# Five raw weight buffers, a first norm with channel factors as 128x8 values, and another order at the phase boundaries

## The chip, the core and the metric

The kernel runs on one core of a Trainium2 chip. The metric is the device time of one execution in microseconds (us), the median of some runs. Four compute engines matter: TensorE (PE in the profile; PEld are its weight loads), VectorE (DVE), ScalarE (ACT) and GpSimd (POOL). SyncE (SP) issues almost every DMA. Each engine works through its own instructions strictly in their order; semaphores order the engines among each other.

## The reference, cut to what matters

Everything is float32, x is 256 tokens of 1024 channels. Two layers of a first block with three branches, then two layers of a second block (a mixer and a feed-forward network):

```python
def first_block(x, mem, ...):
    for l in range(DEPTH):
        h = rms_norm(x, norm_g[l])
        q_a, k_a, v_a, q_h, f_h, i_h, q_m, z = split(h @ w_in[l])
        o_a = moba_attention(rope(norm(q_a)), rope(norm(k_a)), v_a)   # 8 heads of 64
        o_h = rms_norm(hgrn2_chunkwise(q_h, f_h, i_h, lb[l]), hgrn_o_norm[l])
        kv_m = rms_norm(mem, mem_norm_g[l]) @ w_mem_kv[l]             # mem: 256 x 1024
        k_m, v_m = split(kv_m)
        o_m = memory_attention(norm(q_m), norm(k_m), v_m)             # 4 heads of 128
        x = x + (concat([o_a, o_h, o_m]) * silu(z)) @ w_out[l]
    return x

def second_block(x, ...):
    for l in range(DEPTH):
        m = hybrid_mixer(rms_norm_2(x, mix_pre_norm[l]), ...)         # delta net, retention, pooling
        x = x + rms_norm_2(m, mix_post_norm[l])
        h = rms_norm_2(x, ffn_pre_norm[l])
        x = x + rms_norm_2((silu(h @ gate[l]) * (h @ up[l])) @ down[l], ffn_post_norm[l])
    return x
```

`rms_norm(x, g)` divides each token's row by its root mean square and multiplies by the channel gain `g`. Since `mem` is the same for both layers, the two memory norms differ only in that gain.

## The kernel before, in words

**Tiling.** x is two tiles of 128 tokens. A norm makes `xn` of a tile, TensorE transposes it against the identity (8 blocks of 128x128, written into two PSUM banks `mx`), and the result is split into a rounded part and a remainder, `aTh` and `aTl`: that is `hT`, the input of the next phase. Weights come in units of 512 KB (128x1024), 420 in all. Each unit is requested by SP into a buffer `raw`, split into `wh` (a cast on ScalarE) and `wl = raw - wh` (a subtraction on VectorE), and each product is three matmuls, high by high, low by high, high by low, summed in a PSUM bank `acc` or `mx`. The number behind `raw`, `wh`, `wl` in a name is the unit's.

**The weight stream** (class `Stream`, L228 to L327). There are RAW = 3 raw buffers and SLOTS = 6 split buffers; units marked so may take up to SPARE = 2 more from the pool `k4`. `pump` (L292) requests the next raw unit as soon as an earlier raw buffer's second split is issued (`n_dma - n_l < RAW`), and issues splits up to AHEAD = 6 units ahead while a slot is free. `take` hands a unit to the matmuls, `free` gives its slot back.

**The order** is made while the program is built, by a planner (class `Order`, L149, with `Engine`, L98). It keeps an estimate of TensorE's time and of when each tile will be ready, from costs per engine. Work that depends on other work (norms, evacuations, attention, softmaxes) is written as generators that yield what they wait for. After every three matmuls `poll` runs each generator whose tile is due within SLACK = 200 ns of TensorE's estimate, so its instructions fall in there. `join` moves the estimate forward until a named generator is done. The estimate decides only the order in each queue; the real waits are semaphores.

**Phases.** `tok` (L577) makes token-tile outputs, first tile 0 for all keys, then tile 1. `chan` does the same by channels. `out_proj` (L629) sums a product over several units into four banks, two for each tile; its last SKEW units run for tile 0 first and then for tile 1, so that tile 0's residual, norm and transposes can run under tile 1's matmuls. In layer 0 of the first block the order is i_h, f_h, q_h, q_a, k_a, v_a, km, vm, q_m, z1, z0, z2; in layer 1 km and vm come first. The memory is normed once in each layer (`mem_norm`, L811) and `mem_kv` makes its keys and values. The two HGRN chains (`hgrn`, L954; `hZ` is a decayed operand of its matmuls, made after a `TENSOR_TENSOR_SCAN`) and the four softmaxes (`softmax_pv`, L1028, two of MoBA and two of the memory) run as generators beside the projections.

**Start** (`run`, L1710). SP requests x's two tiles, the identity, the gain row `norm_g` broadcast to 128 partitions, then weight units 0, 1, 2. `norm` (L509) squares a tile (`junk`, with the sum as a side output), makes `r` (the small steps `y`), multiplies the tile by `r` and the gain (`xn`, L109 is the helper that records every planned operation), and transposes it.

The gain multiplication and the stream's pace setters in code:

```python
        for xc, gc in zip(self.halves(x), self.halves(gb)):
            xn.append(self.k2([P, 512], "xn"))
            self.dve.scalar_tensor_tensor(xn[-1], xc, r, gc, op0=ALU.mult, op1=ALU.mult)
...
        while self.n_dma < len(self.units) and self.n_dma - self.n_l < self.RAW:
            self._dma()
        if (self.n_h < min(self.n_dma, self.at + self.AHEAD) and self._can_place()
                and o.when(self.raw[self.n_h]) <= o.pe + o.SLACK):
            self._split_h()
```

## Time and profile before

| what | us |
|---|---|
| time before, median of 3 runs (1424.21 to 1426.77) | 1424.57 |
| the profiled execution, whole time | 1426.05 |
| its span in the profile | 1424.3 |
| TensorE busy (97% of the span) | 1386.4 |
| VectorE busy (71%) | 1014.8 |
| ScalarE busy (58%) | 832.2 |
| GpSimd busy (2%) | 23.7 |

The profiled execution takes 1.75 us more than its span, and 1.48 us more than the median of the runs. The profile is read from the whole to the part: the busy time of each engine, the same by stretches of the span, then in a stretch what each engine waited for. A busy time tells nothing of the clock, so the granted clock (PEclk, as a share of full speed) is read beside it.

### The profile page before, as it was taken

What the parts mean: (1) busy time and instruction counts of PE and PEld (TensorE: products, weight loads), DVE (VectorE), ACT (ScalarE), POOL (GpSimd) and SP (SyncE); (2) the same over time, 40 slices, a digit from 0 to 9 for tenths busy, and PEclk for the clock granted to TensorE, in tenths of its full rate; (3) what the DMA queues carried; (4) which work ended last, traced back from release to release, by engine and by line L of the source; (5) the groups of instructions that cost most, each with busy time, mean ns of one, the idle gap of its engine ahead of it and who ended that gap; (6) DMA issues with size and microseconds to landing.
All of it is one profiled execution on the core that took longest, in us unless ns stands there. A gap on an engine that the chain in (4) does not pass through costs nothing.

```text
span 1424.3 us, 20430 instructions
## 1 busy us (share of the span) xinstructions
PE 1386.4 (97%) x7620; PEld 1167.8 (82%) x7620; DVE 1014.8 (71%) x1693; ACT 832.2 (58%) x1415; POOL 23.7 (2%) x65
## 2 busy tenths in 40 slices
PE   7999999999999999999999999999999999999998
PEld 6778887888887898888877888779888887788886
DVE  5887778589777698657777655677958677765554
ACT  5856666576675476556656554555656556555453
POOL 6000000000000000000000000000000000000000
PEclk9999999999999999999999999999999999999999
DMA  8752555554257464235664666745543366566662
GB/s 273 163 179 60 150 191 192 178 155 142 77 155 247 127 180 136 84 104 177 186 221 141 193 190 193 222 120 150 168 126 118 91 193 220 162 191 192 181 190 89
DMA packets 139524, 231.67 MB, mean 163 GB/s; under 512 B 26272, under 2 KB 32032, under 8 KB 139424
## 3 DMA queue, kind: packets, MB, share of 16 engines
q1 hardware_dynamic: 139392, 230.36, 53.6%
q8 instruction: 60, 0.98, 0.3%
q14 instruction: 40, 0.33, 0.1%
q0 software_dynamic: 32, 0.00, 0.0%
HBM read 229.28 MB, written 1.05 MB: 162 GB/s over the span
## 4 chain that ended last, share of the span: by engine, by line
PE 74%; DVE 9%; DMA 9%; ACT 5%; issue 3%; SPq 0%; DVEq 0%; ACTq 0%
PE acc L135 52%; PE mx L135 18%; PE mx L145 4%; DVE wl L109 4%; DMA raw<-in_w_in 3%; ACT wh L109 3%; DMA raw<-in_w_out 2%; DMA raw<-in_ffn_down 1%; DMA raw<-in_ffn_up 1%; ACT sg L109 1%; DVE aTl L109 1%; ACT junk L109 0%; DMA mem<-in_mem 0%; DVE zc L109 0%; DMA x<-in_x 0%
## 5 line engine op out<-in xcount | busy, mean ns | idle before, releaser
L109 DVE TENSOR_TENSOR wl<-raw,wh 128x1024 fp32r<-128x1024 f32 x412 | 502.5, 1222 | 196.6 <-ACT wh L109 191.7
L109 ACT CAST wh<-raw 128x1024 fp32r<-128x1024 f32 x412 | 431.2, 1049 | 258.1 <-PE acc L135 80.8
L135 PE MATMUL acc<-wh,aTh 128*128 128x512 f32 x1232 | 492.5, 400 | 2.3 <-ACT aTh L109 2.3
L135 PE MATMUL acc<-wh,aTl 128*128 128x512 f32 x1232 | 485.4, 394 | 1.2 <-DVE aTl L109 1.2
L135 PE MATMUL acc<-wl,aTh 128*128 128x512 f32 x1232 | 485.8, 394 | 0.2 <-DVE wl L109 0.2
L135 PEld LDWEIGHTS acc<-wh,aTl 128*128 128x128 f32 x1232 | 231.9, 188 | 50.4 <-DVE aTl L109 2.9
L135 PEld LDWEIGHTS acc<-wh,aTh 128*128 128x128 f32 x1232 | 232.4, 189 | 47.9 <-ACT aTh L109 3.1
L135 PEld LDWEIGHTS acc<-wl,aTh 128*128 128x128 f32 x1232 | 232.4, 189 | 45.8 <-issue 1.0
L135 PE MATMUL mx<-wh,ff 128*128 128x512 f32 x352 | 112.6, 396 | 0.0
L135 PE MATMUL acc<-aTh,wh 128*128 128x256 f32 x320 | 91.1, 285 | 0.0
L135 PE MATMUL acc<-aTl,wh 128*128 128x256 f32 x320 | 90.6, 283 | 0.0
L135 PE MATMUL acc<-aTh,wl 128*128 128x256 f32 x320 | 90.5, 283 | 0.0
L135 PEld LDWEIGHTS mx<-wh,ff 128*128 128x128 f32 x352 | 66.3, 190 | 13.5
L109 ACT ACTIVATE sg<-sg 128x512 f32<-128x512 f32 (+1 forms) x120 | 73.9, 615 | 1.7
L109 ACT ACTIVATE sg<-zc 128x512 f32<-128x512 f32 (+1 forms) x60 | 36.9, 614 | 63.5 <-DVE zc L109 63.5
L135 PE MATMUL mx<-wl,ff 128*128 128x512 f32 x176 | 69.2, 393 | 0.0
L135 PEld LDWEIGHTS acc<-aTh,wh 128*128 128x128 f32 x320 | 61.3, 192 | 0.3
L135 PEld LDWEIGHTS acc<-aTh,wl 128*128 128x128 f32 x320 | 61.3, 192 | 0.2
L135 PEld LDWEIGHTS acc<-aTl,wh 128*128 128x128 f32 x320 | 61.3, 192 | 0.0
L109 DVE TENSOR_SCALAR zc<-acc 128x512 f32<-128x512 f32 (+1 forms) x48 | 31.8, 662 | 22.5 <-PE acc L135 22.5
L109 ACT CAST aTh<-mx 128x512 fp32r<-128x512 f32 x52 | 28.9, 585 | 26.2 <-PE mx L145 25.9
L135 PEld LDWEIGHTS mx<-wl,ff 128*128 128x128 f32 x176 | 33.5, 190 | 7.1
(304 smaller groups left out, 1588.5 us busy)
## 6 DMA issues: line engine op xcount, KB each, us to landing
raw<-in_w_in SPq DMA_DIRECT2D x200, 512.0 KB, 4.1
raw<-in_ffn_down SPq DMA_DIRECT2D x44, 512.0 KB, 4.7
raw<-in_w_out SPq DMA_DIRECT2D x40, 512.0 KB, 4.8
raw<-in_ffn_gate SPq DMA_DIRECT2D x40, 512.0 KB, 4.3
raw<-in_ffn_up SPq DMA_DIRECT2D x40, 512.0 KB, 3.9
raw<-in_w_mem_kv SPq DMA_DIRECT2D x16, 512.0 KB, 4.6
raw<-in_w_branch_pool SPq DMA_DIRECT2D x8, 512.0 KB, 4.5
raw<-in_w_branch_ret SPq DMA_DIRECT2D x8, 512.0 KB, 4.7
```

The lines of the kernel that those rows point to most:

```text
L109: r = f(out, *args, **kw)
L135: self._ns.matmul(out, lhsT, rhs, **kw)
L145: self._ns.transpose(out, x, ident)
```

## The change

- **Sizes.** Five raw buffers instead of three, paid for by one buffer less in the pool `k4` and two less in `k2`. SKEW is 4 instead of 3.
- **Planner.** A scan counts twice its columns, and an instruction whose bias or scale is a tile counts 70 ns more.
- **First norm of x.** It multiplies by `r` alone. Its gain comes as a 128x8 tile `gain0` (channel k*128+p at partition p, column k, fetched by GpSimd's queue), and since the transposed blocks have channels on partitions, the gain is the scale of the split: eight ScalarE copies of 128x128 for `aTh` and eight VectorE operations for `aTl` of each tile, where there were two and two.
- **Memory.** It is normed once, without a gain. The gains of both layers come as 128x8 tiles `memgain0` and `memgain1` and go into the splits of the 16 memory weight units, two halves of 512 columns each. Layer 0 makes the keys and values of both layers.
- **Layer order.** i_h, v_a, f_h, q_h, q_a, k_a, then (layer 0) both layers' km and vm, then q_m, z1, z0, z2; in layer 1 i_h and v_a are taken together for each token tile. The units of i_h and v_a may use spare places.
- **One at a time.** `alone` lets the two HGRN generators run one after the other in their middle part, and the four softmaxes one after the other.
- **Start.** x's tile 0, the identity, the memory factors, units 0 and 1, then x's tile 1.
- **Boundary of the first block's layers.** The next norm no longer waits until all of `out_proj`'s matmuls are issued (`proj`).

The instructions in the program change as follows: TensorE's matmuls 6922 to 6906 (16 transposes of the memory less), ScalarE 1321 to 1332, VectorE 1695 to 1708, DMAs issued by SP 490 to 487, and one more by GpSimd.

```diff
-K4, K2, SM, ACC = 12, 24, 24, 3
-SKEW, URGENT = 3, 4
+K4, K2, SM, ACC = 11, 22, 24, 3
+SKEW, URGENT = 4, 4
...
-            self._at = at + self._fixed + self._per * n + (o.ACCUM if "accum_out" in kw else 0.0)
+            per = self._per * (2.0 if name == "tensor_tensor_scan" else 1.0)
+            extra = (o.ACCUM if "accum_out" in kw else 0.0) + sum(o.SCALAR for k in ("bias", "scale") if hasattr(kw.get(k), "tensor"))
+            self._at = at + self._fixed + per * n + extra
...
-    RAW, SLOTS, SPARE, AHEAD = 3, 6, 2, 6
+    RAW, SLOTS, SPARE, AHEAD = 5, 6, 2, 6
...
-        self.o.act.copy(h[:, :w], self.raw[i][:, :w])
+        gain = self.gain(i)
+        if gain is None:
+            self.o.act.copy(h[:, :w], self.raw[i][:, :w])
+        else:
+            for k in range(2):
+                c = slice(k * w // 2, (k + 1) * w // 2)
+                self.o.act.activation(h[:, c], self.raw[i][:, c], AF.Copy, scale=gain[:, k : k + 1])
...
-        self.o.dve.tensor_tensor(self.l[i][:, :w], self.raw[i][:, :w], h.bitcast(F32), op=ALU.subtract)
+        gain = self.gain(i)
+        if gain is None:
+            self.o.dve.tensor_tensor(self.l[i][:, :w], self.raw[i][:, :w], h.bitcast(F32), op=ALU.subtract)
+        else:
+            for k in range(2):
+                c = slice(k * w // 2, (k + 1) * w // 2)
+                self.o.dve.scalar_tensor_tensor(self.l[i][:, c], self.raw[i][:, c], gain[:, k : k + 1], h[:, c].bitcast(F32),
+                                                op0=ALU.mult, op1=ALU.subtract)
...
+            if gb is None:
+                self.dve.tensor_scalar(xn[-1], xc, r, None, op0=ALU.mult)
...
+            yield [tp[b]] + ([gc] if gc is not None else [])
+            if gc is None:
+                self.act.copy(hT[b][0][d], tp[b])
+                continue
+            for k in range(4):
+                g = gc[:, 4 * b + k : 4 * b + k + 1]
+                h, l = (y[:, k, t * P : (t + 1) * P] for y in hT[b])
+                self.act.activation(h, tp[b][:, k, :], AF.Copy, scale=g)
+                self.dve.scalar_tensor_tensor(l, tp[b][:, k, :], g, h.bitcast(F32), op0=ALU.mult, op1=ALU.subtract)
...
+    def alone(self, what):
+
+
+        self.uid += 1
+        mine = f"{what}{self.uid}"
+        last, self.last[what] = self.last.get(what), mine
+        yield last
+        return lambda: self.o.done.add(mine)
...
-            if t == 1:
-                self.o.done.add(f"proj{self.ph}")
...
+        def mem(m):
+            for n, c0 in (("km", 0), ("vm", 512)):
+                for i in range(4):
+                    u.append((((m, n), i), rows(a["w_mem_kv"][m], 256 * i, c0, 2, 512), False, (m, i)))
...
-        for n in (("km", "vm") if l else ()) + ("i_h", "f_h", "q_h", "q_a", "k_a", "v_a") + (() if l else ("km", "vm")):
-            cols(n)
+        for n in ("i_h", "v_a", "f_h", "q_h", "q_a", "k_a"):
+            cols(n, n in ("i_h", "v_a"))
+        if l == 0:
+            for m in range(self.depth1):
+                mem(m)
...
-        self.tok(hT, [(l, "v_a")], lambda key, t, ps: self.evac(v_sb[:, t, :], ps))
         if not l:
-            kmT, vm = self.mem_kv(l, mem)
+            self.kv = [self.mem_kv(m, mem) for m in range(self.depth1)]
+        kmT, vm = self.kv[l]
...
+        leave = yield from self.alone("hgrn")
...
+        leave = yield from self.alone("softmax")
...
+        load_x(0)
+        self.load(self.ident, a["c_ident"])
+        gc = self.cst([P, KD], "gain0")
+        self.nc.gpsimd.dma_start(gc, a["norm_g" if self.depth1 else "mix_pre_norm_2"][0].rearrange("(k p) -> p k", p=P))
+        o.ready[gc.name] = 4000.0
...
+            self.mem_gain.append(self.cst([P, KD], f"memgain{l}"))
+            self.load(self.mem_gain[l], a["mem_norm_g"][l].rearrange("(k p) -> p k", p=P))
...
+        for _ in range(2):
+            self.stream._dma()
+        load_x(1)
...
-                        if ph + 1 < self.depth1:
-                            state["mem"] = self.new_hT()
-                            self.mem_norm(ph + 1, state["mem"])
...
-                wait = self.named_wait(f"proj{ph}") if ph + 1 < self.depth1 else iter(())
                 new, gb = state["hT"], state["gb"]
-                return lambda t, ss: self.chain(wait, self.norm(self.x[t], gb, new, t, ss))
+                return lambda t, ss: self.norm(self.x[t], gb, new, t, ss)
```

**ScalarE at the start of the program**, after the first tile's `y` steps in both. `x0` and `x1` are x's tiles, `ss` the sum of squares, `mx` a PSUM bank of transposed blocks, `aTh` the two halves of `hT`. Before:

```order
L109 ACTIVATE junk_37_200,ss_36_199<-x1_2_86 128x512
L109 ACTIVATE junk_39_203,ss_38_202<-x1_2_86 128x512
L109 ACTIVATE y_43_208<-ss_38_202,b_40_205 128x1
L109 ACTIVATE y_43_208<-y_43_208 128x1
L109 CAST wh0_240<-raw0_172 128x1024
L109 CAST aTh_15_162<-mx_49_221 128x4x128
L109 CAST aTh_17_164<-mx_50_229 128x4x128
L109 CAST wh1_260<-raw1_174 128x1024
L109 CAST aTh_15_162<-mx_53_244 128x4x128
```

After:

```order
L109 CAST wh0_200<-raw0_168 128x1024
L109 ACTIVATE aTh_17_164<-mx_36_216,gain0_4_91 128x128
L109 ACTIVATE aTh_19_166<-mx_37_221,gain0_4_91 128x128
L109 CAST wh1_213<-raw1_170 128x1024
L109 ACTIVATE junk_39_227,ss_38_226<-x1_2_86 128x512
...
L109 ACTIVATE junk_41_230,ss_40_229<-x1_2_86 128x512
L109 ACTIVATE aTh_19_166<-mx_37_221,gain0_4_91 128x128
L109 ACTIVATE y_45_235<-ss_40_229,b_42_232 128x1
...
L109 CAST wh2_260<-raw2_176 128x1024
...
L109 CAST wh3_266<-raw3_178 128x1024
L109 ACTIVATE aTh_17_164<-mx_54_316,gain0_4_91 128x128
```

The squares of tile 1 moved behind two weight splits, and the one copy of each bank became four scaled ones (left out here are the further copies and small steps between; from the split of unit 0 to the last row, the first copy of tile 1, there are 17 instructions).

**SP at the start of the program**, the order of its requests. Before:

```order
L374 DMA x0_1_85<-in_x 128x512 x2
L374 DMA x1_2_86<-in_x 128x512 x2
L374 DMA ident_3_92<-in_c_ident 128x128
L374 DMA gain_14_160<-in_norm_g 128x1024
L250 DMA raw0_172<-in_w_in 128x2x512
L250 DMA raw1_174<-in_w_in 128x2x512
L250 DMA raw2_176<-in_w_in 128x2x512
```

After:

```order
L398 DMA x0_1_85<-in_x 128x512 x2
L398 DMA ident_3_87<-in_c_ident 128x128
L398 DMA memgain0_7_98<-in_mem_norm_g 128x8x1
L398 DMA memgain1_8_100<-in_mem_norm_g 128x8x1
L253 DMA raw0_168<-in_w_in 128x2x512
L253 DMA raw1_170<-in_w_in 128x2x512
L398 DMA x1_2_86<-in_x 128x512 x2
L253 DMA raw2_176<-in_w_in 128x2x512
L253 DMA raw3_178<-in_w_in 128x2x512
L253 DMA raw4_180<-in_w_in 128x2x512
```

Tile 1 moved behind units 0 and 1, the broadcast gain is gone, the two memory factors stand ahead of unit 0, and units 3 and 4 are requested before any further constant.

**TensorE at the boundary of the first mixer and its ffn**, the end of the mixer's `out_proj` for tile 1 (bank `mx_1147` before, `mx_1136` after), the transposes of tile 0's new `xn`, and the first matmuls of the ffn (unit 200 and on). Before:

```order
L135 MATMUL mx_1147_7491<-wh199_7495,aTh_1131_7350 128x512
L135 MATMUL mx_1147_7491<-wl199_7496,aTh_1131_7350 128x512
L135 MATMUL mx_1147_7491<-wh199_7495,aTl_1132_7351 128x512
L145 MATMUL mx_1203_7701<-ident_3_92,xn_1179_7665 128x128 x4
L145 MATMUL mx_1204_7706<-ident_3_92,xn_1180_7667 128x128 x4
L135 MATMUL acc_1216_7738<-wh200_7517,aTh_1151_7565 128x512
L135 MATMUL acc_1216_7738<-wl200_7518,aTh_1151_7565 128x512
L135 MATMUL acc_1223_7797<-wh204_7638,aTh_1151_7565 128x512
```

After:

```order
L137 MATMUL mx_1136_7518<-wl198_7446,aTh_1115_7327 128x512
L137 MATMUL mx_1136_7518<-wh198_7445,aTl_1116_7328 128x512
L147 MATMUL mx_1167_7640<-ident_3_87,xn_1165_7624 128x128 x4
L147 MATMUL mx_1168_7645<-ident_3_87,xn_1166_7626 128x128 x4
L137 MATMUL mx_1136_7518<-wh199_7455,aTh_1115_7327 128x512
L137 MATMUL mx_1136_7518<-wl199_7456,aTh_1115_7327 128x512
L137 MATMUL mx_1136_7518<-wh199_7455,aTl_1116_7328 128x512
...
L137 MATMUL acc_1191_7689<-wh200_1150_7547,aTh_1131_7513 128x512
L137 MATMUL acc_1191_7689<-wl200_1151_7548,aTh_1131_7513 128x512
L137 MATMUL acc_1205_7761<-wh204_7615,aTh_1131_7513 128x512
L137 MATMUL acc_1205_7761<-wl204_7616,aTh_1131_7513 128x512
```

The transposes stood directly ahead of the ffn's first matmul; now the six matmuls of unit 199 for tile 1 stand between.

## Rows read from the trace of the kernel before

**Rows 1.** The page: busy time of the engines, and issues of one DMA.
```profile
PE 1386.4 (97%) x7620; PEld 1167.8 (82%) x7620; DVE 1014.8 (71%) x1693; ACT 832.2 (58%) x1415; POOL 23.7 (2%) x65
...
raw<-in_w_in SPq DMA_DIRECT2D x200, 512.0 KB, 4.1
```
**Rows 2.** By stretch: us, busy (instructions) by engine, PEclk, DMA, GB/s.
```profile
40.00:80.00 40.00, 34.95 (x204) 28.93 (x202) 33.98 (x66) 31.23 (x73) 0.26 (x1) 1.00 0.70 147
...
180.00:240.00 60.00, 58.73 (x275) 47.40 (x274) 45.49 (x69) 36.43 (x60) 0.00 (x0) 1.00 0.61 200
...
400.00:460.00 60.00, 58.58 (x275) 47.46 (x274) 46.59 (x62) 37.57 (x53) 0.00 (x0) 1.00 0.66 203
...
700.00:760.00 60.00, 56.57 (x254) 45.54 (x253) 44.05 (x74) 34.58 (x60) 0.00 (x0) 0.97 0.65 200
...
910.00:950.00 40.00, 36.60 (x157) 28.98 (x156) 28.09 (x57) 22.71 (x46) 0.00 (x0) 0.96 0.60 184
...
1180.00:1240.00 60.00, 57.16 (x262) 46.09 (x261) 45.16 (x75) 34.81 (x59) 0.00 (x0) 1.00 0.69 219
...
1400.00:1424.30 24.30, 17.33 (x78) 13.67 (x76) 10.49 (x27) 5.98 (x18) 0.00 (x0) 0.93 0.12 44
```
**Rows 3.** Timeline, the start: start us, us, what, [idle before <-releaser].
```profile
4.24 0.63 ACT L109 ACTIVATE junk<-x 128x512 bf16<-128x512 f32 x1 [0.15 <-DMA x<-in_x]
...
9.20 2.74 DVE L109 SCALAR_TENSOR_TENSOR xn<-x,r,gain 128x512 f32<-128x512 f32 x4
...
10.02 3.67 PE L145 MATMUL mx<-ident,xn 128*128 128x128 f32 x16 [10.02 <-DVE xn L109]
...
10.41 1.05 ACT L109 CAST wh<-raw 128x1024 fp32r<-128x1024 f32 x1 [1.64 <-DMA raw<-in_w_in]
...
14.34 0.57 PE L135 MATMUL acc<-wh,aTl 128*128 128x512 f32 x1
```
**Rows 4.** Copies scaled by a tile `lay`: ns min/median/max, first and last start, forms.
```profile
L109 ACT ACTIVATE py<-mx,lay x8: 464/471/477, 556.8 to 1044.3; 128x256 f32<-128x256 f32 x8
L109 ACT ACTIVATE aTh<-mx,lay x4: 680/684/689, 687.5 to 1172.3; 128x512 fp32r<-128x512 f32 x4
```
**Rows 5.** Timeline of SP's queue around 60.
```profile
53.34 4.32 SPq L374 DMA_DIRECT2D lay<-in_dn_conv  x3
...
72.50 5.23 SPq L250 DMA_DIRECT2D raw<-in_w_in  x3
```
**Rows 6.** Timeline, ScalarE at 713, in the first mixer's end.
```profile
713.37 1.06 ACT L109 CAST wh<-raw 128x1024 fp32r<-128x1024 f32 x1 [2.71 <-DMA raw<-in_w_out]
```
**Rows 7.** Timelines of SP, ScalarE and TensorE around 745, first mixer to ffn.
```profile
741.94 2.88 SPq L250 DMA_DIRECT2D raw<-in_ffn_up  x3
...
745.59 1.05 ACT L109 CAST wh<-raw 128x1024 fp32r<-128x1024 f32 x1 [2.00 <-DMA raw<-in_ffn_up]
...
745.75 1.29 PE L145 MATMUL mx<-ident,xn 128*128 128x128 f32 x8 [0.41 <-DVE xn L109]
...
747.75 0.50 PE L135 MATMUL acc<-wh,aTh 128*128 128x512 f32 x1 [0.71 <-ACT aTh L109]
```
**Rows 8.** Timeline of TensorE around 925, and that stretch's busy time and clock.
```profile
922.62 0.39 PE L135 MATMUL mx<-wl,ff 128*128 128x512 f32 x1
922.85 0.62 PE L135 MATMUL mx<-wh,ff 128*128 128x512 f32 x2
...
925.67 0.41 PE L145 MATMUL mx<-ident,f 128*128 128x128 f32 x2 [1.98 <-DVE f L109]
...
926.63 0.63 PE L135 MATMUL mx<-wl,ff 128*128 128x512 f32 x1
927.05 1.05 PE L135 MATMUL mx<-wh,ff 128*128 128x512 f32 x2
...
926.00:928.00 2.00, 2.00 (x7) 1.51 (x6) 0.42 (x1) 0.37 (x1) 0.00 (x0) 0.52 0.86 238
```
**Rows 9.** TensorE's waits from 300 to 320: us in total, times, longest.
```profile
PE mx L135 <- DVE hZ L109: 2.8, 1, 2.8
```
**Rows 10.** Timeline of TensorE, the softmaxes of layer 1: first and last matmuls.
```profile
342.87 0.59 PE L135 MATMUL mx<-neg_bf,ident_bf 128*128 128x512 bf16 x2
...
400.14 1.05 PE L135 MATMUL mx<-vm,pT 128*128 128x128 f32 x8
```

More of the change, by code (lines that the diff above doesn't have):

```diff
@@ L280, in _split_h, with gain @@
         w = math.prod(self.shape(i)[1:])
-        self.o.act.copy(h[:, :w], self.raw[i][:, :w])
-        self.n_h += 1
+        gain = self.gain(i)
[5 more added lines that the diff above has]
+                self.o.act.activation(h[:, c], self.raw[i][:, c], AF.Copy, scale=gain[:, k : k + 1])
+        self.n_h += 1
+    def gain(self, i):
+        if len(self.units[i]) < 4:
+            return None
+        m, k = self.units[i][3]
+        return self.kb.mem_gain[m][:, 2 * k : 2 * k + 2]
     def _split_l(self):
@@ L341, in __init__ @@
         self.ph = 0
+        self.last = {}
     def pool(self, name, bufs=1, **kw):
@@ L507, in halves, with norm @@
         return [x[:, n * i : n * i + n] for i in range(2)]
-    def norm(self, x, gb, hT, t, ss=None):
+    def norm(self, x, gb, hT, t, ss=None, gc=None):
         if ss is None:
@@ L514, in norm @@
         r = yield from self.rms_rstd(ss)
-        yield gb
+        if gb is not None:
+            yield gb
         d = (slice(None), slice(None), slice(t * P, (t + 1) * P))
         xn, tp = [], []
-        for xc, gc in zip(self.halves(x), self.halves(gb)):
+        for i, xc in enumerate(self.halves(x)):
             xn.append(self.k2([P, 512], "xn"))
-            self.dve.scalar_tensor_tensor(xn[-1], xc, r, gc, op0=ALU.mult, op1=ALU.mult)
+            if gb is None:
+                self.dve.tensor_scalar(xn[-1], xc, r, None, op0=ALU.mult)
+            else:
+                self.dve.scalar_tensor_tensor(xn[-1], xc, r, self.halves(gb)[i], op0=ALU.mult, op1=ALU.mult)
         for b in range(2):
@@ L524, in norm @@
         for b in range(2):
-            yield tp[b]
-            self.act.copy(hT[b][0][d], tp[b])
-        for b in range(2):
+            yield [tp[b]] + ([gc] if gc is not None else [])
[7 more added lines that the diff above has]
+                self.dve.scalar_tensor_tensor(l, tp[b][:, k, :], g, h.bitcast(F32), op0=ALU.mult, op1=ALU.subtract)
+        for b in range(2 if gc is None else 0):
             yield hT[b][0]
@@ L787, in units1, with cols @@
         u = []
-        def cols(n):
-            w, c0 = (a["w_mem_kv"][l], {"km": 0, "vm": 512}[n]) if n in ("km", "vm") else (a["w_in"][l], self.B1_COLS[n])
+        def cols(n, spare=False):
             for i in range(4):
-                u.append((((l, n), i), rows(w, 256 * i, c0, 2, 512), False))
+                u.append((((l, n), i), rows(a["w_in"][l], 256 * i, self.B1_COLS[n], 2, 512), spare))
+        def mem(m):
+            for n, c0 in (("km", 0), ("vm", 512)):
+                for i in range(4):
+                    u.append((((m, n), i), rows(a["w_mem_kv"][m], 256 * i, c0, 2, 512), False, (m, i)))
         def wo(brs, skew):
@@ L809, in proj_order, with mem_norm @@
         return [u + (i,) for u in units[:n0] for i in range(2)] + [u + (i,) for i in range(2) for u in units[n0:]]
-    def mem_norm(self, l, mT):
-        gb = self.gain(self.a["mem_norm_g"][l])
+    def mem_norm(self, mT):
         for m in range(NT):
             mem = self.load(self.k4([P, D], "mem"), self.a["mem"][0, m * P : (m + 1) * P, :])
-            first = self.named_wait(f"mT{l}0") if m else iter(())
-            self.o.spawn(self.chain(first, self.norm(mem, gb, mT, m)), f"mT{l}{m}")
+            first = self.named_wait("mT0") if m else iter(())
+            self.o.spawn(self.chain(first, self.norm(mem, None, mT, m)), f"mT{m}")
     def km_evac(self, m, ps, kmT, gqk):
@@ L839, in mem_kv, with layer1 @@
         return kmT, vm
[L841 removed]
+    def layer1(self, l, hT, nxt):
         a, o = self.a, self.o
[L844 to L845 removed]
         on = {}
[L847 to L848 removed]
+        io = {"i_h": self.k4([P, NT, G], "i_sb"), "v_a": self.k4([P, NT, G], "v_sb")}
+        i_sb, v_sb = io["i_h"], io["v_a"]
+        for ns in ([["i_h", "v_a"]] if l else [["i_h"], ["v_a"]]):
+            self.tok(hT, [(l, n) for n in ns], lambda key, t, ps: self.evac(io[key[1]][:, t, :], ps))
         if not l:
             o.spawn(self.constants(), "const")
[L851 removed]
+            mem = self.new_hT()
+            self.mem_norm(mem)
         A, kx, qx = ([self.k2([P, 2, S], n) for _ in range(2)] for n in ("hA", "hk", "hq"))
@@ L1712, in run, with load_x @@
         self.setup()
-        for t in range(NT):
+        self.ident = self.cst([P, P], "ident")
+        def load_x(t):
             for h in range(2):
@@ L1724, in run @@
             self.eps[e] = t
+        self.mem_gain = []
+        for l in range(self.depth1):
+            self.mem_gain.append(self.cst([P, KD], f"memgain{l}"))
+            self.load(self.mem_gain[l], a["mem_norm_g"][l].rearrange("(k p) -> p k", p=P))
         self.rope_tables()
@@ L1728, in run @@
         units = sum((self.units1(l) for l in range(self.depth1)), []) + sum((self.units2(l) for l in range(self.depth2)), [])
-        gb = self.gain(pre[0])
         hT = self.new_hT()
         self.ph = -1
+        self.stream = Stream(self, units)
+        for _ in range(2):
+            self.stream._dma()
+        load_x(1)
+        o.ready[self.x[0].name], o.ready[self.x[1].name] = 4200.0, 8500.0
         for t in range(NT):
-            o.spawn(self.norm(self.x[t], gb, hT, t), f"h0{t}")
-        self.stream = Stream(self, units)
+            o.spawn(self.norm(self.x[t], None, hT, t, gc=gc), f"h0{t}")
         o.pump = self.stream.pump
```

17 lines of the change are left out of this document (5 added, 12 removed).

## The prediction

> **What bounds the kernel now.** I read the busy times of the page first: TensorE works 1386.4 of 1424.3 us [rows 1], so a change can give back only the 37.9 us in which it stands still, instructions it no longer has, and time at a lower clock. Next the busy time by stretch, where the reader is to see that this idle time lies in a few places [rows 2]: 5.05 us in 40 to 80 (40.00 less 34.95), 1.27 in 180 to 240, 1.42 in 400 to 460, 3.43 in 700 to 760, 3.40 in 910 to 950, 2.84 in 1180 to 1240, 6.97 in the end piece; 2.8 more is one wait for `hZ` in 300 to 320 [rows 9], and the first 10.02 us have no TensorE work at all [rows 3]. Together that is 37.2. Last I read what ended each wait.
>
> At 713, 745 and 923 the pattern is one. A unit's first split (`wh`, ScalarE) waits for its raw weights: 2.71 us at 713 [rows 6], 2.00 at 745 [rows 7]. Both engines take instructions in their order, so what stands behind that split (on VectorE the remainder `wl`, then the norm or the gate) comes late, and TensorE waits for transposes of it: before 745.75 for `xn`, 0.41, before 747.75 for the `aTh` made of them, 0.71 [rows 7], before 925.67 for `f`, 1.98 [rows 8]. The raw units of 745 were requested at 741.94, three at once [rows 7]. After 1.98 us of idleness the matmuls start 0.42 us apart (926.63 to 927.05) where they had started 0.23 apart (922.62 to 922.85); the granted clock of that stretch is 0.52 of full, so the 1.2 GHz level [rows 8]. Over 700 to 760 the mean is 0.97, over 910 to 950 0.96 [rows 2]: 0.03 x 60 = 1.8 and 0.04 x 40 = 1.6 us lost beside the idle time.
>
> **The change, part by part.** The sum is made against the profiled execution, 1426.05 us, 1.5 above the median of the runs.
>
> Start. Before, `xn` waits for the broadcast gain at 9.20 [rows 3] and the matmuls run on end from 14.34; 16 transposes and 2 matmuls lie before, some 2.2 us of work, so 12.1 us are lost. After, x's first tile, `ident` and two channel-factor loads stand before unit 0. Between x's second half being there (4.24) and unit 0 (10.41), three 512 KB transfers landed: 2.06 us each [rows 3], so unit 0 would land at 6.3 without the factors. Theirs are 4-byte pieces like the three `dn_conv` loads that hold SP for 4.32 us [rows 5], 1.44 each: bounds 6.3 and 9.2, taken 7.5, since two such loads need not hold the queue for their full time. But ScalarE's order puts, ahead of the first piece of tile 1 that TensorE wants in its 15th row, four casts (1.05 each [rows 3]), nine scaled copies of 128 columns, two squares (0.63) and two one-column steps. The scaled copy takes 0.471 for 256 columns and 0.684 for 512 [rows 4]; the same slope gives 0.36 for 128, an estimate. 4.2 + 3.2 + 1.3 + 0.5 = 9.2, so the stream runs on end from about 17.0 (15 to 20). By then 12 transposes and 11 matmuls are done, 3.8 us: 13.2 lost. That is +1.1; with matmuls at the lower level among waits up to +1.8 more. **+1.5** taken (-1 to +6).
>
> 40 to 80. Here SP is busy with small loads: the three `dn_conv` loads from 53.34, and weights are next requested at 72.50 in a group [rows 5]. The loads now lie between weight requests up to the 29th unit, and two more raw buffers are two units of cover, 12 matmuls x 0.23 = 2.7 us each, 5.4 in all, more than those 4.32. **-4.0** (-5.0 to -1: SP still issues them all).
>
> Norm of the memory once: 16 transposes go (at most 1.29/8 = 0.16 each [rows 7], 2.6 in all; nothing if they lay in a gap): **-2.0**. The 16 memory units are split in two halves with a factor: ScalarE 2 x 0.684 [rows 4] against 1.05, +0.3 each, VectorE the like, both less than the 2.7 us a unit takes on TensorE, with ScalarE 58% busy and VectorE 71% [rows 1]: nothing, +5 if that cover fails. Two broadcasts less and two rows more on SP: nothing by themselves.
>
> Boundaries, the 4 skewed units and five buffers. In the order, mixer to ffn, the `xn` transposes stand 42 matmuls behind the end of tile 0's sums (42 x 0.23 = 9.7 us), where before they stood 36 behind (8.3), and 6 matmuls now follow them before the first use of the new `hT`, where before the use followed at once. The late chain of 745 missed by 0.41, then 0.71; 1.4 + 1.4 more is enough for it, even if the raw waits stayed. With five buffers, a unit is requested two units (5.4 us) earlier than the 741.94 of now, more than the waits of 2.71 and 2.00. So 700 to 760: 3.0 of 3.43 idle and half the 1.8 of the clock, **-3.9** (-5 to -1.5); 1180 to 1240, the same place of the second layer, **-2.4** of 2.84 (-2.8 to 0); 910 to 950: 2.0 of 3.40 and 1.4 of the clock, **-3.4** (-4.6 to -1), a part left since nothing there is reordered but the requests; 180 to 240, **-0.6** of 1.27.
>
> `hZ` [rows 9]: the planner now counts the scan double, so it asks for `hZ` later, and the two HGRN chains run one after the other: **-2.3** (-2.8 to 0).
>
> Attention of layer 1. The four softmaxes now stand in a row; before, they ran from 342.87 to 400.14 with overlap [rows 10], 58 us. Serial, they reach in the order through some 72 us of TensorE work into the last `out_proj`, so the end of the layer is nearer to a stall: 1.42 idle [rows 2] can go, or up to 5 come: **+1.0** (-1.4 to +5). New small waits at other reordered rows: **+1.5** (0 to +4; no row of before shows them, the nearest are the 0.41 and 0.71 of [rows 7]).
>
> Sum: 1.5 - 4.0 - 2.0 - 3.9 - 2.4 - 3.4 - 0.6 - 2.3 + 1.0 + 1.5 = -14.6. 1426.05 - 14.6 = 1411.4, less 1.5 is **1410** for the median.
>
> **The rivals.** (1) The added buffers buy little. What holds a request back may be the split slots (six, and one spare buffer fewer in their overflow pool now), not the raw buffers; then the waits of 713, 923 and half of 40 to 80 stay and the reordering saves the rest: start +1.5, 40 to 80 -2.0, transposes -2.0, 745 and 1226 -3, `hZ` -2.3, attention +1.0: -6.8, **1418**. For it: a request that came at 741.94 in a group of three, after none for 8 us, looks like a queue that had been full. Against: full of landed units, which two more would let start at once. The Trainium skill bears on this, "DMA: Bandwidth & Descriptors", section "Anatomy of one DMA": one transfer takes 2.0 us and its bytes over 436 GB/s; its fit is for the path of another queue. By it, as an estimate, 512 KB lands in 3.2 us, three in flight give a unit every 1.07 us, faster than TensorE uses them, and two more would buy nothing but in a burst. The trace's median of 4.1 us to landing [rows 1] is longer than that fit, and even so gives 1.4 us a unit; the loss is in the bursts.
>
> (2) What the start and the new order cost takes back what the boundaries give: start +6, small waits +4, boundaries at their low ends (-1.5, -1, 0), 40 to 80 -2, transposes -2, `hZ` -2: +1.5, **1426**, within 0.2%. For it: ScalarE's row of 17 instructions between unit 0 and tile 1.
>
> (3) Slower: the serial softmaxes. Each now waits for the bank of the one before to be read. Place: the end of layer 1's attention, where `out_proj` needs its outputs. The 72 us of work behind which they hide decides: serial running at 1.25 times the overlapped 58 us just fits; at 1.6 times, 93 us, 21 are bare. The other terms return 15.6, so +5.4 is left: **1430**; it is slower than now by 0.2% from 18.5 bare, some 90 us of softmax. Against: the chain has DVE and ScalarE idle within it, and other generators fill TensorE. For: 58 us with two or more at a time.
>
> That the change doesn't do what it says: only in the start, since unit 0 arrives earlier but the stream doesn't begin earlier; it is in the sum.
>
> **How the numbers follow.** Forecast 0.62 (1402 to 1416), rival (1) 0.18, (2) 0.10, (3) 0.10. All the faster side is the first two: faster by over 0.2% (2.9 us, about what a measurement of this kernel can tell from no change) 0.80, within 0.2% 0.10, slower 0.10. The range takes the forecast and rival (1) with 4 us of its own bounds: **1401 to 1422**; left out are (3), most of (2) and a little below 1401.
>
> **What would show it.** By stretch, TensorE's idle time in 700 to 760, 910 to 950 and 1180 to 1240 falls below 1 us each, and no wait of `wh` for raw units above 1 us is left there; the granted clock stays 1.00 in them. In 40 to 80 below 1.5. Matmuls on end from 15 to 20 us, not from 14.34. No wait for `hZ`. It is wrong if those raw waits stay (rival 1), if the stream starts after 20 us (rival 2), or if TensorE waits for `po` or the memory branch ahead of layer 1's last `out_proj` (rival 3).

## The result, and the profile after

The changed kernel took 1415.21 us (median of 4 runs, 1414.19 to 1416.02) against 1424.39 for the kernel before beside it: a ratio of 0.993, 95% interval 0.9915 to 0.9946. The forecast was 1410, range 1401 to 1422, faster: the time lies within the range and on the side forecast, with 9.2 us gained of the 14.6 expected. The profiled execution after took 1414.19 us with a span of 1412.4. Measured again later, beside other runs of the kernel before, the same kernel gave 0.9958 (0.9942 to 0.9974), 6.4 us; the two together put the gain at about 8 us.

The page after, busy time of each engine; then the busy time by stretch, at the places of [rows 2] (from the first mixer on everything is 10 us earlier). Columns as there: us, busy time and instructions of PE, PEld, DVE, ACT and POOL, granted clock, DMA share, GB/s.

```profile
PE 1382.2 (98%) x7604; PEld 1165.6 (83%) x7604; DVE 1015.1 (72%) x1706; ACT 831.0 (59%) x1422; POOL 26.9 (2%) x66
...
raw<-in_w_in SPq DMA_DIRECT2D x200, 512.0 KB, 4.5
```

```profile
40.00:80.00 40.00, 38.51 (x265) 35.50 (x264) 32.09 (x64) 31.68 (x71) 4.23 (x5) 1.00 0.82 182
...
180.00:240.00 60.00, 59.59 (x299) 48.99 (x298) 46.64 (x65) 38.29 (x60) 0.00 (x0) 1.00 0.55 175
...
400.00:460.00 60.00, 58.82 (x304) 48.93 (x303) 47.03 (x81) 31.40 (x59) 0.00 (x0) 1.00 0.55 172
...
690.00:750.00 60.00, 56.93 (x266) 46.37 (x265) 44.43 (x75) 34.96 (x61) 0.00 (x0) 1.00 0.64 209
...
900.00:940.00 40.00, 36.22 (x163) 29.77 (x162) 28.93 (x61) 21.60 (x45) 0.00 (x0) 0.96 0.55 183
...
1170.00:1230.00 60.00, 57.16 (x263) 46.57 (x262) 45.31 (x75) 35.10 (x61) 0.00 (x0) 1.00 0.67 215
```

Read against [rows 1, 2]: TensorE is busy 4.2 us less (16 transposes less, and less time at the lower clock, since the granted mean over the first mixer's end went from 0.97 to 1.00; the later profile of the same kernel has 1383.8, 2.6 less), and idle 30.2 us instead of 37.9. The idle time went in 40 to 80 (5.05 to 1.49), 180 to 240 (1.27 to 0.41), and at `hZ` (one wait of 2.8 became one of 1.0). At the three boundaries on which the forecast rested most it did not go: 3.43 to 3.07 at the first mixer's end, 3.40 to 3.78 before the second mixer, 2.84 to 2.84 at the second mixer's end. The surprise is that their raw waits did go. ScalarE's waits of `wh` for raw weights, by weight matrix (us in total, times, longest), the longest ones, first before, then after:

```profile
ACT wh L109 <- DMA raw<-in_w_in: 56.9, 43, 3.1
...
ACT wh L109 <- DMA raw<-in_w_out: 24.1, 20, 2.8
```

```profile
ACT wh L109 <- DMA raw<-in_ffn_gate: 9.2, 3, 3.9
...
ACT wh L109 <- DMA raw<-in_w_out: 8.6, 7, 1.6
...
ACT wh L109 <- DMA raw<-in_w_in: 7.2, 4, 3.7
```

Over all matrices that is 136 us in 106 waits before and 30 us in 17 after, and TensorE is no better off at the places where they were read.

### The profile page after: what moved, and what is told of

The parts are those of the page before. It is cut to its first block, busy times and chain, and to the rows that moved or that the text cites. A ratio compares the mean times of both kernels' runs of the same rounds, so it can differ in the third digit from the quotient of the medians.

```text
span 1412.4 us, 20434 instructions
## 1 busy us (share of the span) xinstructions
PE 1382.2 (98%) x7604; PEld 1165.6 (83%) x7604; DVE 1015.1 (72%) x1706; ACT 831.0 (59%) x1422; POOL 26.9 (2%) x66
## 4 chain that ended last, share of the span: by engine, by line
PE 86%; DVE 5%; DMA 4%; issue 2%; ACT 2%; SPq 0%; DVEq 0%; ACTq 0%
PE acc L137 59%; PE mx L137 23%; PE mx L147 5%; DVE wl L109 2%; DMA raw<-in_w_out 1%; ACT wh L109 1%; DMA raw<-in_ffn_gate 1%; DMA mem<-in_mem 0%; DMA raw<-in_w_in 0%; DVE hlf L109 0%; SPq L398 0%; DVE hA L109 0%; DMA memg<-in_mem_k_norm 0%; DMA alogdtb<-in_dn_A_log 0%; DVE y L109 0%
## 5 line engine op out<-in xcount | busy, mean ns | idle before, releaser
L109 DVE TENSOR_TENSOR wl<-raw,wh 128x1024 fp32r<-128x1024 f32 x396 | 480.7, 1221 | 143.7 <-ACT wh L109 138.1
L109 ACT CAST wh<-raw 128x1024 fp32r<-128x1024 f32 x396 | 412.6, 1049 | 167.1 <-PE acc L137 84.2
L109 ACT CAST ff<-mx 128x256 fp32r<-128x256 f32 x44 | 14.4, 375 | 53.0 <-PE mx L147 53.0
L109 ACT CAST aTh<-mx 128x512 fp32r<-128x512 f32 x44 | 24.6, 585 | 30.4 <-PE mx L147 30.4
```

Source lines behind the costliest of these rows:

```text
L109: r = f(out, *args, **kw)
```

## What TensorE waits for now

In the stretch before the second mixer it waits once, for `xn`, and VectorE's timeline shows why (start us, us, what, idle before and its releaser). The rows run from the end of tile 0's residual (`x`) to the transposes of its next norm:

```profile
918.52 1.42 DVE L109 SCALAR_TENSOR_TENSOR x<-yg,r,x 128x512 f32<-128x512 f32 x2
919.86 1.22 DVE L109 TENSOR_TENSOR wl<-raw,wh 128x1024 fp32r<-128x1024 f32 x1
...
921.12 1.22 DVE L109 TENSOR_TENSOR wl<-raw,wh 128x1024 fp32r<-128x1024 f32 x1
922.25 0.21 DVE L109 TENSOR_SCALAR v<-ss,c 128x1 f32<-128x1 f32 x1
922.57 2.36 DVE L109 TENSOR_TENSOR wl<-raw,wh 128x1024 fp32r<-128x1024 f32 x2
924.85 0.21 DVE L109 SCALAR_TENSOR_TENSOR w<-y,v 128x1 f32<-128x1 f32 x1
...
925.05 1.22 DVE L109 TENSOR_TENSOR wl<-raw,wh 128x1024 fp32r<-128x1024 f32 x1
...
926.25 1.22 DVE L109 TENSOR_TENSOR wl<-raw,wh 128x1024 fp32r<-128x1024 f32 x1
927.38 1.41 DVE L109 SCALAR_TENSOR_TENSOR xn<-x,r,gain 128x512 f32<-128x512 f32 x2
```

```profile
928.27 1.94 PE L147 MATMUL mx<-ident,xn 128*128 128x128 f32 x8 [3.78 <-DVE xn L109]
```

Six `wl` of 1.2 us each stand between steps of 0.2 us, 7 us in all in a norm whose end TensorE needs. Before, three stood there, with three raw buffers, and three stand there again in the changed kernel when it has three (the first experiment below): the fourth to sixth are there because their raw units had landed. In the 3 us after TensorE's wait the clock was granted at half, the 1.2 GHz level:

```profile
928.00:931.00 3.00, 2.73 (x10) 2.40 (x11) 2.96 (x9) 1.33 (x3) 0.00 (x0) 0.52 0.97 345
```

At the first mixer's end TensorE waits for `y`, twice. At the second of these two waits, ScalarE's order, from the program, is:

```
L109 CAST wh197_7402<-raw197_7336 128x1024
L109 CAST aTh_1113_7325<-mx_1122_7377 128x4x128
L109 CAST wh200_1150_7547<-raw200_7375 128x1024
L109 CAST aTh_1113_7325<-mx_1125_7417 128x4x128
L109 CAST wh198_7445<-raw198_7345 128x1024
```

Unit 200 goes to a spare place in `k4` and stands ahead of 198 and 199, which have no split slot yet as the program is put in order (that reason is read from the program, not measured). In the kernel before all 412 splits stand in the order of their units; in the changed one 17 stand ahead of an earlier unit's, at 15 places. In the trace that cast (711.60) waits for unit 200's own landing, with unit 198 there since 709.0 (requested at 702.32, landed 6.69 us later):

```profile
711.60 1.05 ACT L109 CAST wh<-raw 128x1024 fp32r<-128x1024 f32 x1 [3.92 <-DMA raw<-in_ffn_gate]
```

```profile
712.68 1.23 DVE L109 TENSOR_TENSOR wl<-raw,wh 128x1024 fp32r<-128x1024 f32 x1 [1.94 <-ACT wh L109]
713.83 0.68 DVE L109 TENSOR_TENSOR y<-y,sig 128x512 f32<-128x512 f32 x1
```

```profile
714.66 0.63 PE L147 MATMUL mx<-ident,y 128*128 128x128 f32 x4 [1.91 <-DVE y L109]
```

It is the chain of [rows 6] again, with a longer wait at its head.

## Experiments

Each group ran beside the kernel before on one chip; its median was 1425.17, 1422.48 and 1422.82 us in the three groups, so kernels of different groups are compared by their ratios. **Theory A** is the prediction's: five raw buffers remove the raw waits and so the stalls. **Theory B**: the buffers gain at some places and lose as much at others, and something else in the change brings the gain.

**Three raw buffers in the changed kernel.**

```diff
-    RAW, SLOTS, SPARE, AHEAD = 5, 6, 2, 6
+    RAW, SLOTS, SPARE, AHEAD = 3, 6, 2, 6
```

> The changed kernel with three raw buffers instead of five, nothing else. Theory A (as the prediction has it: the buffers bring most of what the boundaries gave): waits of wh for raw units of 2 to 3 us come back near 704, 735, 923 and 1190, and the time rises by 5 to 8 us to 1420 to 1423. Theory B (the new order brings it, and five buffers gain at some places and lose at others, since in the changed program 15 splits stand ahead of those of earlier units and five or six stand inside the norm at 924): within 2 us of 1415, with the waits at 704, 712, 1185 and 1193 of another kind, and the 3.9 us at 924 down to below 2.5.

1416.66 us (5 runs), ratio 0.9938 (0.9923 to 0.9953), where the changed kernel has 0.993 and 0.9958. The raw waits of ScalarE are back (137 us in 111 waits); the time differs by no more than the intervals allow, some 2 us. At 924's place TensorE now waits 1.4 us for `f` and 2.1 for `xn`, `aTh` and `aTl`, together nearly the 3.8 of the six splits. Theory A falls for the changed kernel.

**Five raw buffers in the kernel before,** with the pools of the change.

```diff
-K4, K2, SM, ACC = 12, 24, 24, 3
+K4, K2, SM, ACC = 11, 22, 24, 3
...
-    RAW, SLOTS, SPARE, AHEAD = 3, 6, 2, 6
+    RAW, SLOTS, SPARE, AHEAD = 5, 6, 2, 6
```

> The kernel before with the sizes of the change: five raw buffers, 11 buffers in k4, 22 in k2; its order else as before. Theory A: the raw waits at 713, 745, 923 and 1199 go, 6 to 8 us, 1416 to 1418. Theory B: they go, but splits placed ahead of earlier units' hold ScalarE at 713 and 1199 and splits inside the norms lengthen them, so that 2 to 4 us are left of it: 1420 to 1422.

1425.42 us (11 runs), ratio 1.000 (0.9988 to 1.0011): nothing, less even than theory B left. (Five buffers with the old pools were not tried, so a loss by the smaller pools that hides a gain is not excluded here. The experiment before this one changes the raw buffers alone.) By stretch:

```profile
40.00:80.00 40.00, 39.25 (x255) 33.26 (x254) 36.94 (x75) 33.34 (x79) 1.14 (x2) 1.00 0.74 152
80.00:180.00 100.00, 96.32 (x624) 80.26 (x624) 75.96 (x162) 60.65 (x139) 0.00 (x0) 0.98 0.40 125
700.00:760.00 60.00, 55.53 (x258) 44.51 (x257) 45.16 (x75) 34.09 (x62) 0.00 (x0) 1.00 0.61 192
910.00:950.00 40.00, 36.22 (x164) 29.73 (x163) 30.20 (x63) 22.33 (x46) 0.00 (x0) 0.96 0.48 161
```

In 40 to 80 the forecast of the buffers holds in part: 5.05 us idle become 0.75, but 1.9 of the 5.05 were a wait for `hZ`, which only lies further on now. The next stretch, which had 0.07 before, gets 3.68. TensorE's waits there (us in total, times, longest); those for `pT` and `kn` are new:

```profile
PE mx L135 <- DVE pT L109: 2.0, 1, 2.0
PE mx L145 <- DVE kn L109: 0.9, 1, 0.9
PE mx L135 <- DVE hZ L109: 0.8, 1, 0.8
```

The wait of [rows 9], 2.8 us between 300 and 320 before, is 1.0 in this run:

```profile
PE mx L135 <- DVE hZ L109: 1.0, 1, 1.0
```

And 700 to 760 and 910 to 950 have more idle time than before (4.47 and 3.78 against 3.43 and 3.40), the second by the same six splits.

**The splits in unit order.** Each cast is queued behind the one before it.

```diff
-            self.o.act.copy(h[:, :w], self.raw[i][:, :w])
+            ins = self.o.act.copy(h[:, :w], self.raw[i][:, :w])
+            if self.last_h is not None:
+                self.kb.tc.add_manual_dep(ins.ins, self.last_h, mybir.DependencyInfo(
+                    mybir.DependencyClass.NoSync, mybir.DependencyReason.DATA), reason="unit order")
+            self.last_h = ins.ins.name
```

> The changed kernel, in which each cast wh on ScalarE is queued behind the cast of the unit before it, so no split stands ahead of an earlier unit's. Theory B: TensorE's waits for y at 704, 712, 1185 and 1193 (6.5 us together) fall below 2.5, the time to 1410 to 1412; the 3.9 us at 924 stays, since its splits are in order already. Rival: those waits come from raw units that land late whatever stands first: they stay, and the time stays within 1.5 us of 1415.

1414.87 us (6 runs), ratio 0.9936 (0.9913 to 0.9959): no change. From 690 to 770 the wait for `y` halves, from 3.1 us to 1.5, and new ones take its place (TensorE's waits: us in total, times, longest):

```profile
PE mx L147 <- DVE y L109: 1.5, 2, 1.0
PE mx L147 <- DVE xn L109: 0.8, 1, 0.8
PE acc L137 <- ACT aTh L109: 0.7, 1, 0.7
```

So the queue jump makes the waits for `y`, as read, but it does not cost the time: what the splits do not delay there they delay in the norm behind, where five `wl` stand ahead of `xn` in this run and three in the changed kernel.

**Seven split buffers instead of the two raw ones.**

```diff
-    RAW, SLOTS, SPARE, AHEAD = 5, 6, 2, 6
+    RAW, SLOTS, SPARE, AHEAD = 3, 7, 2, 6
```

> The changed kernel with three raw buffers and seven split buffers, about the same memory as five and six. If split buffers are what holds the stream back (the prediction's first rival): 1409 to 1413, with the splits of 268 on before the norm at 924 rather than in it. If raw buffers are: 1419 to 1422, raw waits of over 2 us near 704 and 1190.

1430.28 us (6 runs), ratio 1.0026 (1.001 to 1.0042): slower than the kernel before, outside both expectations, and 13.6 us above the run with three raw and six split buffers. The loss lies mostly in the first block, where the planner's order came out otherwise; of TensorE's waits from 70 to 180 and from 400 to 430 the first rows are

```profile
PE mx L137 <- DVE hZ L109: 5.7, 2, 4.2
```

```profile
PE mx L147 <- DVE y L109: 3.6, 1, 3.6
```

The first follows a memory unit's split on VectorE that waited 3.33 us for its `wh`. It says nothing for or against slots as such; it says how far one size moves the order.

**Fewer splits inside a norm.** While a norm at a phase boundary is outstanding, the planner issues no split and no request once the second splits are URGENT units ahead of the matmuls.

```diff
-SKEW, URGENT = 4, 4
+SKEW, URGENT = 4, 2
```

> The changed kernel with URGENT 2 instead of 4: while a norm of a boundary is due, splits are issued only up to two units ahead. At 924 three wl stand on VectorE ahead of xn instead of six. Theory B (five raw buffers landed early let splits of 1.2 us each stand inside the norm, and xn is late by them): 3 x 1.2 = 3.7 us less, so the 3.9 us wait there falls below 1.5 and the time to 1411 to 1413. Rival: the splits are only pushed behind the norm, TensorE then waits for wl as long: idle time moves, 1414 to 1417.

1413.19 us (6 runs), ratio 0.9934 (0.992 to 0.9948). At the boundary the expectation holds: three `wl` ahead of `xn`, a wait of 0.8 us instead of 3.8.

```profile
PE mx L147 <- DVE xn L109: 0.8, 1, 0.8
PE acc L137 <- ACT aTh L109: 0.2, 1, 0.2
```

Whether the whole is faster than the changed kernel this run can't tell by itself (0.993 and 0.9958 for that, measured beside other groups).

**SKEW back to 3.**

```diff
-SKEW, URGENT = 4, 4
+SKEW, URGENT = 3, 4
```

> The changed kernel with SKEW 3 as before. If the fourth skewed unit is what removed the waits for xn and aTh at the boundaries of mixer and ffn (0.6 + 0.9 + 0.5 us at 745 and as much at 1226 in the kernel before): they come back, +3 to +4, 1418 to 1419. Rival, they went because the splits behind the late raw units no longer stand in the norm's way: within 1.5 us of 1415.

1420.12 us (12 runs), ratio 0.9985 (0.9975 to 0.9994). Half or more of the gain is gone with this one number. At the first mixer's end TensorE waits again at the start of the ffn:

```profile
738.64 1.29 PE L147 MATMUL mx<-ident,xn 128*128 128x128 f32 x8 [0.78 <-DVE xn L109]
...
741.67 0.50 PE L137 MATMUL acc<-wh,aTl 128*128 128x512 f32 x1 [0.41 <-DVE aTl L109]
```

These are 1.2 us, and as much at the second mixer's end; but the waits for `y` are 0.7 shorter at each place (2.4 and 2.1 for 3.1 and 2.8). In all the idle time rises by 0.8 us from 690 to 770 and by 0.7 from 1160 to 1250, so these places account for some 1.5 us of the 0.27 to 0.55% lost, which are 3.8 to 7.8 us.

**SKEW 4 alone in the kernel before.**

```diff
-SKEW, URGENT = 3, 4
+SKEW, URGENT = 4, 4
```

> The kernel before with SKEW 4 instead of 3 and nothing else; three raw buffers. Taking SKEW back in the changed kernel cost 5 to 8 us, more than the 2 x 1.5 us that its two mixer boundaries show. If the fourth skewed unit by itself brings that: 1416 to 1419 against some 1424. If it brings only the waits for xn and aTh at 745 and 1226 (2.0 + 2.1 us): 1420 to 1421. If it needs the five buffers, since with three the raw units come late anyway: within 1.5 us of before.

1417.51 us (12 runs), ratio 0.9972 (0.9957 to 0.9986), 5.3 us by the medians and 4.0 by the ratio, with three raw buffers and ScalarE waiting for raw units as often as before (57.7 us in 45 waits for `w_in` alone). The changed kernel beside it has 0.9958, and the two intervals overlap. So by the two runs the fourth skewed unit brings more than half of the gain, alone (0.28 of 0.42%) and in company. How, the page and three stretches show in part:

```profile
PE 1382.9 (98%) x7620; PEld 1166.7 (82%) x7620; DVE 1017.7 (72%) x1695; ACT 831.1 (59%) x1413; POOL 24.0 (2%) x65
```

```profile
700.00:760.00 60.00, 57.13 (x266) 46.13 (x265) 46.00 (x77) 35.21 (x61) 0.00 (x0) 1.00 0.62 194
910.00:950.00 40.00, 37.32 (x173) 29.82 (x173) 31.75 (x67) 23.13 (x48) 0.00 (x0) 1.00 0.52 168
```

```profile
300.00:320.00 20.00, 17.97 (x100) 13.96 (x98) 17.13 (x30) 16.28 (x43) 0.00 (x0) 0.91 0.42 129
```

The same 7620 matmuls and transposes take 3.5 us less than in [rows 1], and TensorE is idle 4.4 us less (33.6 for 37.9). The clock of the first two stretches is 1.00 where it was 0.97 and 0.96, which gives back 3.4 us; in the third, behind a wait for `hZ` of 2.0 us, it is 0.91 where it was 1.00, which takes 1.8. So clock and idle time both have a part, the clock the smaller one: over all runs its mean is 0.9978 here and 0.9968 in the kernel before beside it, and 0.001 of 1422 us is 1.4. Of the idle time 0.9 us less lie in 180 to 240, 0.6 in 700 to 760 and 0.2 from 1160 to 1250, the places with a skewed `out_proj`; the rest lies where none is, and what one profile shows there differs by some microseconds from the next. Where most of the 4 to 5 us is won is therefore not shown.

**The softmaxes not in series.**

```diff
-        yield last
+        yield None if what == "softmax" else last
```

> The changed kernel whose four softmaxes of a layer need not wait for each other; the two HGRN chains still do. The prediction's third rival (serial softmaxes cost): faster by 1 to 5 us, 1410 to 1414, with less idle time around 400. If the series is hidden: within 1.5 us of 1415. If it protects the PSUM banks that the projections need: slower by 1 to 4.

1415.66 us (6 runs), ratio 0.9949 (0.9935 to 0.9963). TensorE has no idle time from 400 to 460 (60.00 of 60.00, 58.82 in the changed kernel), and the total doesn't show it. The series of the softmaxes costs nothing that can be measured. The series of the HGRN chains was left out in no run.

**x's second tile ahead of the weights.** The calls alone:

```diff
         load_x(0)
+        load_x(1)
...
-        for _ in range(2):
+        for _ in range(3):
             self.stream._dma()
-        load_x(1)
```

The two memory factors are requested behind these units, and the planner's estimate of when tile 1 is there goes from 8500 to 6300 ns.

> The changed kernel with x's second tile requested right behind the first, then the identity, three weight units, and the memory factors behind them. The prediction says that the start costs 1.5 us since tile 1's first piece stands 17 instructions behind unit 0's split on ScalarE. If so, here the squares of tile 1 are done before unit 0 lands and the matmuls run on end from about 15 instead of 17.8: 1412 to 1414. Rival: unit 0 lands 2 us later, matmuls start later by as much and the start is as long: 1415.

1412.63 us (6 runs), ratio 0.9931 (0.9916 to 0.9946). The first of the rows below is the changed kernel's, TensorE's first piece of tile 1, behind which its matmuls run on end, 0.23 to 0.24 us apart; the second is this one's, from which they do so (they have had no wait since 12.14, but started 0.43 us apart).

```profile
17.78 0.50 PE L137 MATMUL acc<-wh,aTh 128*128 128x512 f32 x1 [0.46 <-ACT aTh L109]
```

```profile
16.14 0.39 PE L137 MATMUL acc<-wl,aTh 128*128 128x512 f32 x1
```

That is 1.6 us earlier, with four transposes and one matmul less done by then, so some 1.0 us is won. Whether the whole is faster than the changed kernel this run can't tell by itself either.

**The changed kernel again,** beside the next two kernels and SKEW 4 alone.

> The changed kernel itself, again, beside the others of this group so that they are compared on one chip: 0.993 of the kernel before, within 0.15%.

1416.45 us (7 runs), ratio 0.9958 (0.9942 to 0.9974). Its profile has 3.28 us idle in 40 to 80 where the first had 1.49:

```profile
40.00:80.00 40.00, 36.72 (x254) 33.72 (x254) 30.23 (x61) 29.74 (x68) 2.74 (x5) 1.00 0.81 185
```

So one profile can't size a term there to better than some 2 us.

**Both edits that didn't lose:** URGENT 2, and x's second tile first.

> The changed kernel with URGENT 2 and with x's second tile requested right behind the first, the two edits that did not lose. If what they showed in the profile adds up (3.8 us at 890 to 960, 1.0 at the start, less 2 of new waits at 22 to 80 and 690 to 770): 2 to 3 us faster than the changed kernel. If idle time only moves: within 1 us of it.

1409.35 us (4 runs), ratio 0.9912 (0.9894 to 0.993) beside 0.9958 (0.9942 to 0.9974) for the changed kernel: the intervals don't touch. 7.1 us by the medians, 6.5 by the ratios, more than the 2 to 3 expected. The boundary is what the two show most clearly, the changed kernel's second profile first:

```profile
900.00:940.00 40.00, 36.22 (x154) 29.58 (x153) 28.52 (x58) 21.17 (x44) 0.00 (x0) 0.91 0.59 198
```

```profile
900.00:940.00 40.00, 39.08 (x183) 31.61 (x182) 29.96 (x63) 23.22 (x47) 0.00 (x0) 1.00 0.56 187
```

2.86 us less idle, and a clock of 1.00 instead of 0.91 (0.09 x 40 = 3.6 us; in the changed kernel's first profile it was 0.96, 1.6 us). That is what the six splits cost in these profiles, 4.5 to 6.5 us; the kernel with the two edits is faster than the changed one.

**The same with the splits in unit order.**

> The same as combo2, and each cast wh queued behind that of the unit before it. In order, the waits for y at the mixers' ends (6.5 us) halve, as they did alone; what came in their place alone was a wait for xn at 735 and 1216 (1.9 + 1.7 us), behind splits inside that norm, which URGENT 2 keeps down. If so, 3 to 5 us faster than the changed kernel; if the splits then come too late for the ffn, no faster than combo2.

1409.95 us (4 runs), ratio 0.9913 (0.9895 to 0.9931): no faster than the last. The wait for `y` from 690 to 770 is down to 0.7 us, and `xn` and `aTh` take 1.3, as when the order was pinned alone.

## Why the prediction was right, and where it was not

The time fell into the range; the sum was too large by 5 to 8 of its 14.6 us (9.2 and 6.4 measured), and its largest cause failed. The three boundary terms are 9.7 of the 14.6, and without them the sum would have been 4.9, less than what came. So that 1415 lies this near to 1410 is in part luck.

- **Start, +1.5.** The matmuls ran on end from 17.78 (forecast 17.0), so by the same counting 17.8 - 3.8 = 14.0 us are lost, 1.9 more than before. Two parts were off and cancelled: unit 0's cast began at 9.32, past the bound of 9.2 and well past the 7.5 taken, and ScalarE's row took 8.0 us from there to tile 1's first piece (17.36) where 9.2 were worked out: an instruction starts some 0.1 us before the one ahead ends, which over 17 of them is 1.7. The row does set when tile 1 starts: with it taken apart (x's second tile first) some 1.0 us is won. But TensorE is idle in the first 20 us for 9.4 us, less than the 10.0 before. What is lost more than before is lost by the pace: the matmuls ahead of 17.78 start 0.43 us and more apart, as they did in [rows 8] at half the clock. The prediction had this beside the sum, with up to 1.8.

```profile
14.31 0.63 PE L137 MATMUL acc<-wh,aTh 128*128 128x512 f32 x1
14.74 0.63 PE L137 MATMUL acc<-wl,aTh 128*128 128x512 f32 x1
```

- **40 to 80, -4.0.** Measured -3.6 in one profile and -1.8 in the other. What went is 3.2 us of waits for `xn` and `wl`; what is left, 1.5 and 3.3 us, is all for `hZ`, 1.9 before. The cause, buffers that cover SP's small loads, is not shown. In the kernel before, five buffers leave 0.75 us idle there, but what was won came back in the next 100 us; and the changed kernel with three buffers has 3.00 us there, 0.6 for `xn` and 2.4 for `hZ`, so its order does most of it without the buffers. [rows 5] was also read too shortly: SP requested three weight units between its two rows (at 57.77 and 59.05), and the stretch without a request is the 12 us from 60.5 to 72.5, more than the 5.4 of cover. For the whole that cover brought nothing (ratio 1.000). TensorE's wait for `hZ` there before:

```profile
PE mx L135 <- DVE hZ L109: 1.9, 1, 1.9
```

- **16 transposes, -2.0; `hZ`, -2.3.** The busy time fell by 4.2 and 2.6 in the two profiles, but in the kernel before with SKEW 4, which still has the 16 transposes, by 3.5: their part is not shown by it. The wait for `hZ` fell from 2.8 to 1.0. It fell to 1.0 as well in the kernel before with five buffers, which has neither the planner's new cost nor the HGRN chains one after the other, so the reason given is not shown either.
- **Boundaries, -3.9, -3.4 and -2.4.** This step failed. The prediction put: "With five buffers, a unit is requested two units (5.4 us) earlier than the 741.94 of now, more than the waits of 2.71 and 2.00", and took the stalls of TensorE with the waits. The waits went, 106 to 17; the idle time at the three places stayed at 3.07, 3.78 and 2.84. It did not ask what would be late next: the splits themselves, which came early enough to stand ahead of earlier units' and between the steps of a norm. The buffers measured by themselves: 0.0% in the kernel before, with the smaller pools that pay for them, and nothing beyond the noise in the changed one. Of the three terms only the clock at the first mixer's end came, up to 1.8 us. The fourth and smallest, 180 to 240, did come (1.27 to 0.41 for the forecast -0.6).
- **SKEW.** "1.4 + 1.4 more is enough for it, even if the raw waits stayed" was right, and was the stronger half of that paragraph: in the kernel before, where the raw waits do stay, the fourth unit alone brings 4 to 5 us, of which 0.56 idle and up to 1.8 of the clock lie at the first mixer's end; in the changed kernel, taking it back brings 1.2 us of waits for `xn` and `aTl` there. The prediction had it inside the boundary terms and gave it no price of its own.
- **Attention, +1.0; new small waits, +1.5.** 1.42 idle became 1.18, no new small waits show behind the start, and the serial softmaxes cost nothing: the third rival was rightly small.
- **The rivals.** The first, "added buffers buy little", was what happened, at 1415 and not 1418, but not for its reason: the raw waits it expected to stay went, with the split slots at six. The run with seven slots can't speak for or against it. By the estimate set beside it, worked out from the fit in the Trainium skill, "DMA: Bandwidth & Descriptors", section "Anatomy of one DMA", more transfers in flight would buy nothing but in a burst. The time agrees with that and the landing doesn't: a unit's median landing was 4.5 us after and 4.1 before, above its 3.2, and the added requests did end most of the raw waits. (A unit each 1.07 us would also be 490 GB/s, above the 436 that the estimate starts from; with 1.2 us the argument is the same.) A rival should have been built on the splits' place and not on the requests.

What stays open: where in the kernel most of SKEW's gain lies; what in the rest of the change, SKEW aside, brings the 0.15% (0.06 to 0.25) that the kernel with SKEW 3 keeps, for which the transposes alone could be enough; and whether the kernel before with SKEW 4 and URGENT 2 would do as well as the changed one.

## What to carry to other kernels

A wait on an engine that does not bound the kernel is a symptom until a run without it is faster: 106 us of ScalarE's waits (136 less 30) were bought off with two buffers, and nothing came back that could be told from the noise. Work that is let loose earlier lands somewhere in a queue; before buying an earlier start, look which short steps of a chain stand behind it there, and hold it back at those places. Six more matmuls between a norm and its first use did more than two buffers: 0.28% in the kernel before, where five buffers gave 0.0%.

## What the runs showed of the hardware that was not expected

Waits of about the same length were followed by different clocks: behind 1.98 us of idleness before 925.67 the clock fell [rows 8], behind 1.91 us before 714.66 in the changed kernel matmuls went on at the full pace (715.36 to 715.59, 0.23 apart), behind 3.78 us before 928.27 it fell to 0.52. The same wait of 3.78 us went with a mean clock of 0.96 over 900 to 940 in one profile of the changed kernel and of 0.91 in the other. Idle time of TensorE therefore has no single price; the two levels have to be read from the rows each time.

```profile
715.36 0.39 PE L137 MATMUL acc<-wh,aTh 128*128 128x512 f32 x1
715.59 0.39 PE L137 MATMUL acc<-wl,aTh 128*128 128x512 f32 x1
```

One kernel's time also moved with its mean granted clock: the 18 runs of the kernel before in the last group go from 1418.27 us at 0.999 to 1426.86 at 0.994. So two single profiles can differ by several microseconds with no edit between them.
